# Two-layer encoder: query and key columns of the first four k tiles inside the first pieces, a first modulation unit on TensorE, copies of turned x on ScalarE

## The chip, the core and the metric

The kernel runs on one core of a Trainium2 chip. Its engines work from queues of their own, each in its written order: TensorE multiplies matrices into the accumulation memory (PSUM), VectorE and ScalarE do element-wise work, GpSimd a little, and SyncE (SP) issues nearly all transfers from the main memory. In the profile they are PE (and PEld for loading of weights into TensorE), DVE, ACT, POOL and SP. The metric is the device time of one execution in microseconds (us). Before the change the median of three executions was 2297.42 us (2294.97 to 2298.74).

## The reference

The program is an encoder trunk of two layers over 256 tokens of 2048 channels, all in float32. What matters here is the head of layer 0:

```python
mod = (c_act @ w_mod[l] + b_mod[l]).reshape(bn, 6, d)     # six vectors of 2048
h = layer_norm(x) * (1.0 + scale_m) + shift_m
proj = h @ w_in[l]                                        # 2048 x 4288
uv, q_c, kv_c, k_r, sb, sc, sh, ag = jnp.split(proj, IN_SPLITS, axis=-1)
y_a = gmlp_mixer(uv, ...)          # U and V, 512 columns each
y_b = mla_mixer(q_c, kv_c, k_r, ...)   # B: 704 columns, padded to 768
y_c = short_conv_mixer(sb, sc, sh, ...)  # E = sb (512), C = sc and sh (1024)
y_d = conformer_conv(ag, ...)      # D: 1024 columns
y = jnp.concatenate([y_a, y_b, y_c, y_d], axis=-1) @ w_out[l]
x = layer_norm(ALPHA * x + (1.0 + gate_m) * y, ...)
```

After that comes a gated feed-forward with a width-3 convolution (weights 2048 x 11264 and 5632 x 2048), and the same again for layer 1. Every weight is read once; the modulation alone reads 2048 x 12288 numbers a layer.

## The kernel before, in words

A **k tile** is 128 of the 2048 input channels; there are 16. The input projection multiplies each k tile of the weights with the same k tile of h, transposed (channels on the partitions, 256 tokens along the row; tiles hF), and sums over the 16.

**Modulation on VectorE.** The vectors mod are not made by TensorE. VectorE runs over w_mod, one k tile at a time: acc = w * c_act[k] + acc (mod_step, lines 246 and 248; tiles qacc, macc, sources wmod), and at the end TensorE sums acc over the partitions with products against a column of ones (mod_cols, result ps_mod), to which the bias bcol is added by a product with the identity matrix. ScalarE then copies the few columns out (line 205, and line 86 with +1 for scales).

**Layer 0 starts in five pieces** (PIECES: k tiles 0-1, 2-3, 4-7, 8-11, 12-15; function by_pieces). Shift and scale for a piece's channels are made first (mod_piece: units of 1 MB of w_mod), then h for that piece (line 1477 and line 86 in place on hF), then the piece's share of the products with the columns D, U, V and E, while VectorE makes the modulation of the next piece. The code of a piece has four steps; each does a quarter of D, and the first three one of U, V and E (function side), and between them calls some_mods, which issues the next piece's modulation units. D keeps its four accumulation banks (accD) through all pieces. U, V and E share the two banks that are left: at the end of a side, ScalarE copies both banks out (sums, line 1284; part, line 1289), and from the second piece on VectorE adds what was copied to the sum in SBUF (line 1290; in the last piece line 1286 directly).

**Plain and split products.** For k tiles 0 to 3 (PLAIN_KT = 4), and for U, V and E up to k tile 11, weights go straight from memory into TensorE as float32 (tiles wexact, loads on line 431); each such product shows as two TensorE records. Otherwise the weights (wraw, loads on line 439) and h are split in a high part (whi, hT: ScalarE, lines 453 and 473) and a low part (wlo: VectorE, lines 454 and 474), and three products are summed.

**After the pieces** group B runs over its 16 k tiles in 8 units of 2 (function group, all plain, tiles B_c), then C in the same manner; the attention of B is computed in between C's products. One unit is one call of stream, which issues the unit's loads, a number of w_mod steps for later use (RATES: 1.6 per unit for B; generator mods), and a number of VectorE jobs that wait in the list background (STEPS: 2 per unit for B; they are the 31 taps of D's convolution, line 903, with ScalarE's products of line 902).

**Buffers.** w_mod units, w_mod steps and wraw share four 1 MB tiles (rawp); wexact, whi and wlo share four and four half-MB tiles (splitp). SP issues loads in program order and waits at the first whose tile isn't free. The Tile framework orders each engine's instructions by its own estimate, so the order on an engine is not quite that of the code.

**The start.** x is loaded, normalised (ScalarE, line 86, tiles xn), turned by TensorE (line 1449, ps_xT), and copied into hF by ScalarE (line 1453) and VectorE (line 1455) in turns. At the same time VectorE runs the first piece's 16 modulation steps of 512 columns (four units of four k tiles).

Of the kernel before, what the change touches and what calls it, by code (L numbers as in the profile page):

```python
# [35 lines left out]
    dict(B=1.6, C=1.9, out=1.7, first=1.2, up=0.68, down=0.83),  # L36
# [4 lines left out]
    dict(B=2, C=2, up=2),  # L41
# [13 lines left out]
def encoder_kernel(ctx: ExitStack, tc: tile.TileContext, A: dict, consts: bass.AP, out: bass.AP):  # L55
# [195 lines left out]
    def mod_piece(l, ms, k0, nkt):  # L251
# [5 lines left out]
        units = []  # L257

        def unit(u):
# [9 lines left out]
            for k in range(nk):  # L269
                mod_step(acc, raw[:, k, :, :].rearrange("p m c -> p (m c)"), u * nk + k, u == 0 and k == 0)  # L270
# [4 lines left out]
        def sums():  # L275
            for i, m in enumerate(ms):
                mod_cols(l, m, k0, acc[:, i * width : (i + 1) * width])
# [198 lines left out]
    def group(w, c0, width, name, then, ntm=0, nk=2, hF=None, bg=0, spare=0):  # L476
# [48 lines left out]
        return KT // nk, load, products, end, bg  # L525

    def group2(w, c0, name, then, bg=0, spare=0):
# [23 lines left out]
        return KT // nk, load, products, lambda: then(box["c"]), bg  # L551

    def run(g):
        units, load, products, end, bg = g
        for u in range(units):
            stream(lambda: load(u), lambda item, u=u: products(item, u), bg)
        pending.append(end)
# [685 lines left out]
    def by_pieces(l, w_in, hF, between, mix_d, mix_u, mix_v, mix_b, mix_c, mix_e):  # L1243
# [4 lines left out]
        cols = {"U": C_UV, "V": C_UV + 512, "E": C_SB}  # L1248
# [22 lines left out]
        def side(g, parts, k0, nkt):  # L1271
            ps = [acc_tile(f"{g}{l}_{i}") for i in range(2)]
            for kt, part in parts:
                st, sp = kt == k0, kt == k0 + nkt - 1
                if g == "V":
                    ts = terms(kt, part)
                    for t in range(2):
                        for n, (w, x) in enumerate(ts):
                            mm(ps[t], x[:, t * P : (t + 1) * P], w, st and n == 0, sp and n == len(ts) - 1)
                else:  # L1280
                    chan_major(ps, kt, part, range(4), st, sp)
            for i in range(2):
                if k0 == 0:
                    act.copy(sums[g][i], ps[i])
                elif k0 + nkt == KT:
                    dve.tensor_tensor(out=sums[g][i], in0=ps[i], in1=sums[g][i], op=ALU.add)
                else:
                    part = tmp_tile("part")
                    act.copy(part, ps[i])
                    dve.tensor_tensor(out=sums[g][i], in0=part, in1=sums[g][i], op=ALU.add)  # L1290

        first = between(0)[1]
        first()
        for q, (k0, nkt) in enumerate(PIECES):
# [4 lines left out]
            def load(g, kt):  # L1299

                c0, width = (C_AG, 1024) if g == "D" else (cols[g], 512)
                nk = min(2048 // width, nkt)
# [17 lines left out]
            for s in range(4):  # L1320
# [114 lines left out]
    def normed_T(hF):  # L1435
# [3 lines left out]
        for t in range(2):  # L1439
# [4 lines left out]
            for q in range(4):  # L1444
# [7 lines left out]
                if q % 2 == 0:  # L1452
                    act.copy(dst, src)
                else:
                    dve.tensor_copy(dst, src)
# [151 lines left out]
```

## Time and profile before

| what | value |
|---|---|
| median of three executions | 2297.42 us (2294.97 to 2298.74) |
| the profiled execution, its own time | 2298.88 us |
| its span in the profile | 2297.1 us |
| TensorE, VectorE, ScalarE busy | 97%, 78%, 47% of the span |
| read from memory | 601 MB |

The profiled execution lies 1.5 us over the median, and its span 1.8 us under its own time; the 1.8 us are around the span and not in any view. Times in the views count from the start of the span. A row of grouped instructions gives the line, the engine, the operation, what is written and read with the shape, the count, the busy time, the mean of one, and the idle time of the engine just before them with what ended it. In a table of stretches, each engine has its busy us with the number of instructions that began there, and behind them stand the granted TensorE clock (1.00 is full), the busy share of the 16 transfer engines (transfers that overlap can take it over 1) and the rate in GB/s. TensorE's busy time is that of records that overlap in a pipeline, so the mean of one is longer than its share of a dense stretch: the busy time divided by the count is used here.

### The profile page before, as it was taken

How to read it: one execution, taken by the hardware profiler on the slowest of the kernel's cores; microseconds unless marked ns; L12 is line 12 of the kernel's file. 1: busy time of each engine (PE TensorE's matmuls, PEld its weight loads, DVE VectorE, ACT ScalarE, POOL GpSimd, SP SyncE). 2: the span in 40 equal slices, each digit the busy share in tenths (PEclk: the TensorE clock that was granted, in tenths of full speed). 3: DMA queues.
4: the chain of work that ended last, by engine and by line, in shares of the span. 5: the costliest groups of instructions: out<-in, count | busy, mean ns of one | idle time of the engine just before them, and what ended most of it. 6: DMA issues, size and time to landing. Idle time of an engine off the chain costs nothing.

```text
span 2297.1 us, 31478 instructions
## 1 busy us (share of the span) xinstructions
PE 2238.4 (97%) x12387; PEld 1934.1 (84%) x12387; DVE 1790.7 (78%) x2211; ACT 1071.6 (47%) x1597; POOL 34.4 (1%) x65
## 2 busy tenths in 40 slices
PE   6899999999999999999999999999999999999998
PEld 4688886798888888888789999889888888888886
DVE  6878987778888888998977899796676565565676
ACT  2235742335454544544455435545454454454553
POOL 2000000000000000000000000000000000000000
PEclk9899999999999999999999999999999999999999
DMA  9999788777889888898857677875665555555554
GB/s 344 362 340 343 271 321 333 263 278 279 317 303 335 292 326 318 303 354 307 311 186 260 202 238 252 291 260 185 249 243 202 193 178 197 192 193 185 188 195 147
DMA packets 228717, 605.21 MB, mean 263 GB/s; under 512 B 14660, under 2 KB 27188, under 8 KB 210900
## 3 DMA queue, kind: packets, MB, share of 16 engines
q1 hardware_dynamic: 227784, 602.30, 73.7%
q8 instruction: 97, 1.59, 0.3%
q0 software_dynamic: 784, 0.90, 0.1%
q14 instruction: 52, 0.43, 0.0%
HBM read 601.05 MB, written 2.10 MB: 263 GB/s over the span
## 4 chain that ended last, share of the span: by engine, by line
PE 89%; DVE 5%; DMA 3%; issue 1%; ACT 1%; SPq 0%; POOL 0%; DVEq 0%; POOLq 0%; ACTq 0%
PE g_c L83 21%; PE v_c L83 21%; PE d L83 20%; PE o L83 8%; PE D_c L83 4%; PE C_c L83 4%; PE B_c L83 3%; DMA wmod<-in_w_mod_dram 2%; PE U_c L83 1%; DVE wlo L454 1%; PE U L83 1%; PE E L83 1%; PE ps_mod L83 1%; PE E_c L83 1%; DVE qacc L248 1%
## 5 line engine op out<-in xcount | busy, mean ns | idle before, releaser
L453 ACT CAST whi<-wraw 128x1024 fp32r<-128x1024 f32 (+1 forms) x632 | 643.6, 1043 | 780.4 <-PE g_c L83 210.0
L454 DVE TENSOR_TENSOR wlo<-wraw,whi 128x1024 fp32r<-128x1024 f32 (+1 forms) x632 | 750.6, 1214 | 292.2 <-ACT whi L453 278.3
L83 PE MATMUL d<-whi,a 128*128 128x512 f32 x1344 | 390.6, 392 | 0.9 <-ACT whi L453 0.9
L248 DVE SCALAR_TENSOR_TENSOR macc<-wmod,cact,macc 128x2048 f32<-128x2048 f32 (+2 forms) x174 | 353.8, 2033 | 32.3 <-DMA wmod<-in_w_mod_dram 31.7
L83 PE MATMUL v_c<-hT,whi 128*128 128x512 f32 (+1 forms) x1456 | 343.1, 383 | 0.0
L83 PE MATMUL g_c<-hT,whi 128*128 128x512 f32 (+1 forms) x1344 | 313.3, 380 | 0.0
L83 PEld LDWEIGHTS v_c<-hT,whi 128*128 128x128 f32 x1456 | 264.6, 189 | 48.5
L83 PEld LDWEIGHTS d<-whi,a 128*128 128x128 f32 x1344 | 253.2, 189 | 54.6 <-ACT whi L453 2.2
L83 PEld LDWEIGHTS g_c<-hT,whi 128*128 128x128 f32 x1344 | 243.4, 189 | 43.2
L83 PE MATMUL d<-wlo,a 128*128 128x512 f32 x672 | 234.4, 392 | 1.6 <-DVE wlo L454 1.6
L83 PE MATMUL v_c<-hT,wlo 128*128 128x256 f32 x1400 | 190.7, 283 | 0.0
L83 PEld LDWEIGHTS v_c<-hT,wlo 128*128 128x128 f32 x1400 | 183.1, 191 | 6.6
L83 PE MATMUL g_c<-hT,wlo 128*128 128x256 f32 x1280 | 175.8, 283 | 0.0
L83 PEld LDWEIGHTS g_c<-hT,wlo 128*128 128x128 f32 x1280 | 168.2, 191 | 5.9
L83 PEld LDWEIGHTS d<-wlo,a 128*128 128x128 f32 x672 | 127.0, 189 | 30.3 <-DVE wlo L454 3.9
L473 ACT CAST a<-g 128x512 fp32r<-128x512 f32 x132 | 80.8, 619 | 91.0 <-PE d L83 89.3
L83 PE MATMUL o<-whi,a 128*128 128x512 f32 x384 | 112.4, 398 | 0.8 <-ACT whi L453 0.8
L474 DVE TENSOR_TENSOR a<-g,a 128x512 fp32r<-128x512 f32 x132 | 87.7, 685 | 9.5 <-ACT a L473 9.5
L83 PEld LDWEIGHTS o<-whi,a 128*128 128x128 f32 x384 | 73.1, 191 | 17.5 <-ACT whi L453 1.2
L83 PE MATMUL D_c<-hT,whi 128*128 128x256 f32 x432 | 82.0, 290 | 2.8 <-ACT hT L473 2.3
L248 DVE SCALAR_TENSOR_TENSOR qacc<-wmod,cact,qacc 128x1024 f32<-128x1024 f32 (+1 forms) x75 | 80.3, 1070 | 2.6 <-DMA wmod<-in_w_mod_dram 0.5
L1364 DVE SCALAR_TENSOR_TENSOR u<-g,pf,u 128x254 f32<-128x254 f32 (+1 forms) x176 | 73.5, 476 | 3.0 <-ACT u L86 3.0
(371 smaller groups left out, 2603.7 us busy)
## 6 DMA issues: line engine op xcount, KB each, us to landing
wraw<-in_ffn_w_up_dram SPq DMA_DIRECT2D x168, 1024.0 KB, 5.0
wmod<-in_w_mod_dram SPq DMA_DIRECT2D x134, 1024.0 KB, 6.2
wraw<-in_ffn_w_down_dram SPq DMA_DIRECT2D x88, 1024.0 KB, 5.2
wraw<-in_w_in_dram SPq DMA_DIRECT2D x33, 1024.0 KB, 6.9
wmod<-in_w_mod_dram SPq DMA_DIRECT2D x64, 512.0 KB, 9.2
wraw<-in_w_out_dram SPq DMA_DIRECT2D x26, 1024.0 KB, 6.7
wmod<-in_w_mod_dram SPq DMA_DIRECT2D x32, 768.0 KB, 6.6
wexact<-in_w_in_dram SPq DMA_DIRECT2D x46, 512.0 KB, 7.4
```

The lines of the kernel that those rows point to most:

```text
L83: pe.matmul(o, lhsT, rhs, start=start, stop=stop, skip_group_check=True)
L248: i = dve.scalar_tensor_tensor(out=acc, in0=w, scalar=col, in1=acc, op0=ALU.mult, op1=ALU.add)
L453: act.copy(hi[:, :m], r)
L454: i = dve.tensor_tensor(out=lo[:, :m], in0=r, in1=hi[:, :m].bitcast(F32), op=ALU.subtract)
L473: act.copy(hi, src)
L474: dve.tensor_tensor(out=lo, in0=src, in1=hi.bitcast(F32), op=ALU.subtract)
L1364: dve.scalar_tensor_tensor(out=u[:, sh:], in0=x[:, : S - sh], scalar=col(k, j), in1=u[:, sh:], op0=ALU.mult, op1=ALU.add)
```

## The change

Four things change, all before the end of group B of layer 0, with three numbers of the plan.

1. **Group B's first four k tiles join the first two pieces.** The step that did V does "VB" where the piece is plain: after V, B's 768 columns of the piece's two k tiles are loaded (two transfers of 384 KB a piece, line 440 in the new file, behind V's load and two of the next piece's modulation loads, ahead of E's) and multiplied (12 products a piece, three banks of four blocks, between V's and E's). Their sums stay in SBUF (sumB); group starts with unit 2 of 8 and copies them into its accumulation banks first.
2. **Sides start from their earlier sum.** side now takes its banks one after the other. From the second piece on, ScalarE copies the sum so far into the bank (act.copy(o, total)), TensorE accumulates on top, and ScalarE copies the bank back. VectorE's additions (lines 1286 and 1290, 24 of 128x512) are gone. U's last piece is not copied back: its GELU reads the banks (mix_u moves from behind the pieces into the last one).
3. **The first modulation unit goes to TensorE.** Of the first piece's four units, unit 0 (4 k tiles x 2 vectors x 2 column blocks) becomes 16 products of a 128x128 block of w_mod with a column of c_act, into a bank (modfirst), which then also takes the bias and the sums of VectorE's remaining 12 steps.
4. **All eight copies of turned x are ScalarE's** (line 1468 in the new file).

Of the plan: each of the first three steps of the last piece calls next(mods), which is one w_mod step (1 MB and one VectorE pass of 128x2048); B's rate becomes 1.634 (6 units, 9.8 steps, where 8 units gave 12.8); B's background jobs per unit become 3 (18 where there were 16).

How the order moves is shown at three places. **VectorE at the start** (qacc is the modulation sum, hF the turned x, ps_xT the transposes, bcol the bias); before:

```order
L248 SCALAR_TENSOR_TENSOR qacc<-wmod,cact,qacc 128x512 x4
L1455 COPY hF_116<-ps_xT 128x4x128
L248 SCALAR_TENSOR_TENSOR qacc<-wmod,cact,qacc 128x512
L1455 COPY hF_118<-ps_xT 128x4x128
L248 SCALAR_TENSOR_TENSOR qacc<-wmod,cact,qacc 128x512
L1455 COPY hF_116<-ps_xT 128x4x128
L248 SCALAR_TENSOR_TENSOR qacc<-wmod,cact,qacc 128x512 x2
L1455 COPY hF_118<-ps_xT 128x4x128
L248 SCALAR_TENSOR_TENSOR qacc<-wmod,cact,qacc 128x512
L142 COPY bcol_106<-ps_rows 128x96
L248 SCALAR_TENSOR_TENSOR qacc<-wmod,cact,qacc 128x512 x4
L1477 TENSOR_SCALAR hF_115<-hF_115,mod_1_0_276,mod_0_0_270 128x256
```

and now (rs is the factor of the normalisation, which xn waits for):

```order
L583 SCALAR_TENSOR_TENSOR rs_in_145<-mv_in_143,rs_in_145 128x1
L583 SCALAR_TENSOR_TENSOR rs_in_188<-mv_in_186,rs_in_188 128x1
L246 TENSOR_SCALAR qacc<-wmod,cact 128x512
L248 SCALAR_TENSOR_TENSOR qacc<-wmod,cact,qacc 128x512 x10
L142 COPY bcol_106<-ps_rows 128x96
L248 SCALAR_TENSOR_TENSOR qacc<-wmod,cact,qacc 128x512
L1490 TENSOR_SCALAR hF_115<-hF_115,mod_1_0_289,mod_0_0_284 128x256
```

The four copies have left, 12 modulation steps stand where 16 did, and rs stands ahead of all of them (before, three steps stood ahead of it).

**VectorE in the third piece** (k tiles 4-7; qacc here is the fourth piece's modulation, wlo the low part of D's weights); before:

```order
L246 TENSOR_SCALAR qacc<-wmod,cact 128x1024
L248 SCALAR_TENSOR_TENSOR qacc<-wmod,cact,qacc 128x1024 x7
L1290 TENSOR_TENSOR sumU<-part,sumU 128x512 x2
L248 SCALAR_TENSOR_TENSOR qacc<-wmod,cact,qacc 128x1024 x6
L454 TENSOR_TENSOR wlo<-wraw,whi 128x1024
L1290 TENSOR_TENSOR sumV<-part,sumV 128x512
L454 TENSOR_TENSOR wlo<-wraw,whi 128x1024
```

and now:

```order
L246 TENSOR_SCALAR qacc<-wmod,cact 128x1024
L248 SCALAR_TENSOR_TENSOR qacc<-wmod,cact,qacc 128x1024
L483 TENSOR_TENSOR hT<-hF_116,hT 128x2x256 x2
L248 SCALAR_TENSOR_TENSOR qacc<-wmod,cact,qacc 128x1024 x12
L463 TENSOR_TENSOR wlo<-wraw,whi 128x1024 x2
L248 SCALAR_TENSOR_TENSOR qacc<-wmod,cact,qacc 128x1024 x2
```

The additions that waited for U's and V's banks between the steps are gone; the same 14 steps still stand ahead of the first wlo.

**SP in the last piece** (k tiles 12-15; wraw of 2x1024 is D's weights, of 4x512 that of U, V and E); before:

```order
L439 DMA wraw<-in_w_in_dram 128x2x1024
L439 DMA wraw<-in_w_in_dram 128x4x512 x2
L439 DMA wraw<-in_w_in_dram 128x2x1024
L439 DMA wraw<-in_w_in_dram 128x4x512
```

and now:

```order
L448 DMA wraw<-in_w_in_dram 128x2x1024
L448 DMA wraw<-in_w_in_dram 128x4x512
L358 DMA wmod<-in_w_mod_dram 128x2048
L448 DMA wraw<-in_w_in_dram 128x4x512
L358 DMA wmod<-in_w_mod_dram 128x2048
L448 DMA wraw<-in_w_in_dram 128x2x1024
L448 DMA wraw<-in_w_in_dram 128x4x512
L358 DMA wmod<-in_w_mod_dram 128x2048
```

Two w_mod steps now stand ahead of D's second and E's weights, in the same four tiles.

Behind that, up to the end of layer 0's ffn_w_up, a few neighbouring instructions change places on the engines; from there on every engine's order is the old one. The diff, cut to its core:

```diff
-    dict(B=1.6, C=1.9, out=1.7, first=1.2, up=0.68, down=0.83),
+    dict(B=1.634, C=1.9, out=1.7, first=1.2, up=0.68, down=0.83),
-    dict(B=2, C=2, up=2),
+    dict(B=3, C=2, up=2),
...
-    def mod_cols(l, m, k0, acc):
+    def mod_cols(l, m, k0, acc, begun=None):
-        ps = ms_tile("ps_mod")
-        mm(ps[:, 0:n], ident, bcol[l][:, m * KT + k0 : m * KT + k0 + n], True, False)
+        ps = ms_tile("ps_mod") if begun is None else begun
+        mm(ps[:, 0:n], ident, bcol[l][:, m * KT + k0 : m * KT + k0 + n], begun is None, False)
...
+        begun = acc_tile("modfirst") if k0 == 0 else None
...
             for k in range(nk):
-                mod_step(acc, raw[:, k, :, :].rearrange("p m c -> p (m c)"), u * nk + k, u == 0 and k == 0)
+                kt = u * nk + k
+                if begun is None or u > 0:
+                    mod_step(acc, raw[:, k, :, :].rearrange("p m c -> p (m c)"), kt, kt == (0 if begun is None else nk))
+                    continue
+                for i in range(n):
+                    for j in range(nkt):
+                        o = begun[:, i * nkt + j : i * nkt + j + 1]
+                        mm(o, raw[:, k, i, j * P : (j + 1) * P], cact[:, kt : kt + 1], k + i + j == 0, False)
...
+        skip = 0 if begun is None else PLAIN_KT // nk
...
-            if u == 0:
+            if u == skip:
                 box["c"] = [acc_tile(f"{name}_c{i}") for i in range((ncm + 1) // 2)]
+                if begun is not None:
+                    for bank, part in zip(box["c"], begun):
+                        act.copy(bank, part)
...
         def side(g, parts, k0, nkt):
-            ps = [acc_tile(f"{g}{l}_{i}") for i in range(2)]
-            for kt, part in parts:
...
+            for i, total in enumerate(sums[g]):
+                o = acc_tile(f"{g}{l}_{i}")
+                if k0 > 0:
+                    act.copy(o, total)
+                for kt, part in parts:
...
+                if g == "U" and k0 + nkt == KT:
+                    u_banks.append(o)
                 else:
-                    part = tmp_tile("part")
-                    act.copy(part, ps[i])
-                    dve.tensor_tensor(out=sums[g][i], in0=part, in1=sums[g][i], op=ALU.add)
+                    act.copy(total, o)
+            if u_banks and g == "U":
+                mix_u(u_banks, None)
...
-                if s < 3:
-                    g = "UVE"[s]
+                for g in ("U", "VB", "E", "")[s] if exact else ("U", "V", "E", "")[s]:
                     load(g, k0)
-                    some_mods((0.5, 0.85, 1.0)[s])
+                    some_mods((0.5, 0.85, 1.0, 1.0)[s])
                     side(g, [(kt, loaded[(g, kt)]) for kt in range(k0, k0 + nkt)], k0, nkt)
+                if k0 + nkt == KT and s < 3:
+                    next(mods)
         mix_d(accD, None)
-        mix_u(sums["U"], None)
...
-        run(group(w_in, C_Q, 768, f"B{l}", mix_b, hF=hf, bg=STEPS[l]["B"]))
+        run(group(w_in, C_Q, 768, f"B{l}", mix_b, hF=hf, bg=STEPS[l]["B"], begun=sums["B"]))
...
-                if q % 2 == 0:
-                    act.copy(dst, src)
-                else:
-                    dve.tensor_copy(dst, src)
+                act.copy(dst, src)
```

More of the change, by code (lines that the diff above doesn't have):

```diff
@@ L523, in end @@
             then(box["c"], box["t"])
-        return KT // nk, load, products, end, bg
+        return range(skip, KT // nk), load, products, end, bg
     def group2(w, c0, name, then, bg=0, spare=0):
@@ L549, in load @@
             return weights(w, u * nk, nk, c0, 512, False, spare if u == 0 else 0)
-        return KT // nk, load, products, lambda: then(box["c"]), bg
+        return range(KT // nk), load, products, lambda: then(box["c"]), bg
     def run(g):
         units, load, products, end, bg = g
-        for u in range(units):
+        for u in units:
             stream(lambda: load(u), lambda item, u=u: products(item, u), bg)
```

32 lines of the change are left out of this document (15 added, 17 removed).

## The prediction

> **What bounds the kernel now.** I read the page first, then busy time by stage, then who waited for whom, then the stretches with a low clock.
>
> ```profile
> span 2297.1 us, 31478 instructions
> PE 2238.4 (97%) x12387; PEld 1934.1 (84%) x12387; DVE 1790.7 (78%) x2211; ACT 1071.6 (47%) x1597; POOL 34.4 (1%) x65
> ```
>
> TensorE is busy 97% of the span, so the kernel is a queue of TensorE work; a gain must come from the 59 us in which it is not busy (2297.1 - 2238.4), or from stretches at a low clock. By stage (start; first two pieces; third; fourth; last piece with the rest of D; group B; C):
>
> ```profile
> 0.00:32.50 32.50, 9.99 (x51) 7.96 (x51) 20.71 (x38) 12.10 (x19) 8.95 (x27) 0.93 0.98 327
> 32.50:53.00 20.50, 20.50 (x79) 16.22 (x80) 11.52 (x17) 3.94 (x9) 0.00 (x0) 0.87 1.06 378
> 53.00:85.00 32.00, 25.36 (x104) 18.66 (x102) 27.50 (x32) 7.69 (x15) 5.32 (x10) 0.89 0.98 350
> 85.00:122.50 37.50, 34.94 (x172) 28.80 (x173) 29.63 (x28) 7.93 (x12) 0.00 (x0) 0.91 1.01 370
> 122.50:160.00 37.50, 35.96 (x205) 29.74 (x205) 30.53 (x31) 10.48 (x18) 0.00 (x0) 1.00 0.97 354
> 160.00:190.70 30.70, 30.40 (x232) 29.24 (x231) 23.24 (x22) 11.62 (x14) 0.00 (x0) 1.00 0.79 280
> 190.70:235.20 44.50, 44.17 (x217) 38.86 (x215) 41.61 (x40) 30.07 (x71) 2.56 (x5) 1.00 1.01 369
> 235.20:310.00 74.80, 74.51 (x359) 62.81 (x359) 66.24 (x82) 43.86 (x106) 1.80 (x1) 1.00 0.77 279
> ```
>
> Length less TensorE's busy time: the start costs 22.5 us, the second piece (53 to 85) 6.6, the third and fourth 4.1 together; from 160 on TensorE is full. The transfers are the reverse: full (0.97 to 1.06) up to 160 and in group B, 0.79 in the last piece. So the pieces are bound by transfers with TensorE idle in places, group B by both, the last piece by TensorE alone. The waits inside the pieces, and the half clock that follows a gap:
>
> ```profile
> PE D_c L83 <- DVE wlo L454: 3.4, 2, 2.6
> PE V L83 <- DMA wexact<-in_w_in_dram: 2.7, 2, 2.4
> PE D_c L83 <- ACT hT L473: 2.0, 1, 2.0
> PE E L83 <- DMA wexact<-in_w_in_dram: 2.0, 1, 2.0
> 27.60:37.60 10.00, 7.92 (x24) 6.83 (x25) 7.42 (x12) 1.02 (x3) 0.00 (x0) 0.50 1.09 356
> 67.75:72.30 4.55, 4.55 (x7) 1.97 (x8) 4.44 (x4) 0.01 (x1) 0.00 (x0) 0.62 0.94 325
> 75.15:79.00 3.85, 3.85 (x10) 3.07 (x11) 3.84 (x5) 0.00 (x0) 0.00 (x0) 0.56 1.03 397
> 110.00:113.00 3.00, 3.00 (x14) 3.00 (x15) 3.00 (x4) 0.00 (x0) 0.00 (x0) 0.50 1.02 401
> ```
>
> In the second piece V waits 2.4 us and E 2.0 us for weights. The granted clock falls after the gaps: 4.55 us at 0.62 behind V's wait lose 1.7 us, 3.85 at 0.56 behind E's 1.7, 3.0 at 0.50 behind the wait for wlo 1.5.
>
> **The change part by part.** The sum is made against the profiled execution, 2298.88 us.
>
> *a) The start.* D's first product began at 32.49 us.
>
> ```profile
> 14.37 0.49 DVE L246 TENSOR_SCALAR qacc<-wmod,cact 128x512 f32<-128x512 f32 x1 [0.27 <-DMA wmod<-in_w_mod_dram]
> 16.34 0.22 DVE L569 SCALAR_TENSOR_TENSOR rs_in<-mv_in,rs_in 128x1 f32<-128x1 f32 x2
> 17.76 2.33 DVE L248 SCALAR_TENSOR_TENSOR qacc<-wmod,cact,qacc 128x512 f32<-128x512 f32 x3 [0.53 <-DMA wmod<-in_w_mod_dram]
> L248 DVE SCALAR_TENSOR_TENSOR qacc<-wmod,cact,qacc 128x512 f32<-128x512 f32 x14 | 10.5, 748 | 0.8 <-DMA wmod<-in_w_mod_dram 0.5
> L86 ACT ACTIVATE xn<-x,rs_in 128x512 f32<-128x512 f32 x8 | 6.1, 808 | 12.3 <-DVE rs_in L569 12.3
> L1455 DVE COPY hF<-ps_xT 128x512 f32<-128x512 f32 x4 | 2.8, 688 | 0.3 <-PE ps_xT L1449 0.3
> L1453 ACT COPY hF<-ps_xT 128x512 f32<-128x512 f32 x4 | 2.3, 576 | 0.1
> L83 PE MATMUL ps_mod<-onesR,qacc 128*128 128x1 f32 x48 | 5.5, 245 | 0.0
> 17.40 3.00 PE L1449 MATMUL ps_xT<-cst,xn 128*128 128x128 f32 x12 [12.79 <-ACT xn L86]
> 29.64 1.87 PE L83 MATMUL ps_mod<-onesR,qacc 128*128 128x1 f32 x8 [2.42 <-DVE qacc L248]
> 30.69 0.16 ACT L205 COPY mod<-ps_mod 128x2 f32<-128x2 f32 x1 [6.13 <-PE ps_mod L83]
> 32.49 6.36 PE L83 MATMUL D_c<-hF,wexact 128*128 128x256 f32 x16
> ```
>
> VectorE's 12 remaining steps can't start before unit 1 has landed (17.76); 12 x 0.75 = 9.0 us and the bias's turn bring it to about 27 instead of 29.6 us, the four copies (2.8 us) no longer between. The 16 products on TensorE are 32 records of one column like the sums': 32 x 5.5 / 48 = 3.7 us from 14.37, done at 18.0, hidden as TensorE waits for x until 17.4, so the first transpose is late by 0.6. ScalarE then has 8 copies x 0.58 and about 6 of the 8 normalisations x 0.76 ahead of it from about 18.6: 9.2 us, to 27.8. It is now the later one. From the first modulation copy (30.69) to D was 1.8 us, so D starts at about 29.7: **-2.8 us**. Bounds: -3.5 (rs comes earlier, its row now ahead of three steps), -1 (ScalarE's queue longer by its four copies' waits).
>
> *b) First and second piece.* B's row prices the moved products:
>
> ```profile
> L83 PE MATMUL B_c<-hF,wexact 128*128 128x256 f32 x192 | 41.9, 379 | 0.0
> DVE hF L1477 <- ACT mod L86: 9.8, 3, 8.4
> ```
>
> 24 of 96 products are 48 records x 0.218 = 10.5 us, 5.2 in each piece. The first piece was full, so its 5.2 stand on the path. In the second they stand between V and E, where E's wait (2.0) and its low clock (1.7) go. V's wait stays: its load is queued on SP behind modulation units whose tiles VectorE must free, and VectorE stood 8.4 us at line 1477 for the first piece's end, which moves by a) and the 5.2 us with TensorE. So the third piece's modulation comes by 10.5 - 3.7 = 6.8 us later, less a): +4.0. The transfers give the same: 1.57 MB (four of 393 KB) at 378 GB/s are 4.2 us in stretches that were full. **+6.8 us**; bounds: +2.7 (V's wait and low clock go as well), +10.5 (no wait goes).
>
> *c) Third and fourth piece.* The additions leave VectorE:
>
> ```profile
> DVE sumU L1290 <- ACT part L1289: 7.5, 5, 3.2
> L1290 DVE TENSOR_TENSOR sumU<-part,sumU 128x512 f32<-128x512 f32 x6 | 4.1, 691 | 7.5 <-ACT part L1289 7.5
> L1289 ACT COPY part<-E 128x512 f32<-128x512 f32 x6 | 3.5, 587 | 9.6 <-PE E L83 9.6
> ```
>
> Six additions a group, and 7.5 us in which VectorE, in order, stood at U's and could not run the steps behind it. The wlo that TensorE waited for (3.4 us, with 1.5 of low clock) stood behind those steps. What is late next is D's second weights themselves, as the transfers are 4 us later by b). I take half, **-2.5 us**; bounds 0 and -4.9. The new copies into the banks (0.59 each) lie beside the other bank's products (8 records x 0.218 = 1.7 us in the second piece, 16 or 3.5 us after); without that cover they would cost some 1.3 us a bank, with the copy out.
>
> *d) The last piece.* Three w_mod steps go where transfers are at 0.79 and VectorE at 23.2 of 30.7 us: hidden, 0; bounds 0 and the slower rival. U's additions and copies gone change nothing on TensorE, which is full.
>
> *e) Group B* loses the 10.5 us from a stretch in which TensorE was busy 44.17 of 44.5: **-10.5 us**. The three copies into its banks lie beside D's last products. Transfers lose 1.57 MB and three steps there, so they stay no bound.
>
> *f) Behind B.*
>
> ```profile
> L903 DVE TENSOR_TENSOR convD<-convD,prodD 128x1020 f32<-128x1020 f32 (+12 forms) x13 | 15.5, 1189 | 0.8 <-ACT prodD L902 0.5
> PE ps_mod L83 <- DVE macc L248: 1.8, 1, 1.8
> ```
>
> In the new order 10 taps, not 15, stand ahead of the first use of B's sums on VectorE, so five more stand between the attention's VectorE steps in C: 5 x 1.19 = 5.9 us of VectorE, mostly beside C's products (TensorE had 74.5 of 74.8). And an earlier TensorE meets the modulation of the output projection, where it waited 1.8 us already, earlier. I take **+2.5 us** for both; bounds 0 and +7.7.
>
> Sum: -2.8 + 6.8 - 2.5 + 0 - 10.5 + 2.5 = **-6.5 us**, 2292.4 for the profiled execution. That execution lies 1.5 us over the median of the three, so against 2297.42 it is **2291**.
>
> **The rivals.** *No gain (25%).* The pieces absorb little: the transfers are late by b) through both later pieces, c) gives 0 to 3 us and E's wait returns in another place, b) at its upper bound: -2.8 + 10.5 - 1.5 - 10.5 + 2.5 = -1.8, so about 2296. For it speaks the transfer share of 1.0 in every piece, against it that 4.2 us of transfers can't cost 10.5.
>
> *More gain by the clock (17%).* D's first products ran at 0.50 from 32.49 to 37.6, behind a TensorE that had been idle 2.42 us before the sums and little used before. With products from 14.4 on and transposes until about 28, the idle stretch shrinks to a microsecond or two, and D could start at full clock: 5.1 us x 0.5 = -2.6 us, and with c) at its full 4.9, -11.5 in all, 2286. [...]
>
> *Slower (13%).* The last piece. SP is in order and the four 1 MB tiles are shared; before, all five weight loads were issued by 158.1:
>
> ```profile
> 144.17 13.95 SPq L439 DMA_DIRECT2D wraw<-in_w_in_dram x5
> 170.95 1.05 ACT L453 CAST whi<-wraw 128x1024 fp32r<-128x1024 f32 x1 [1.83 <-PE U L83]
> ```
>
> Now D's second weights wait for a tile that U's splits free, E's for a tile that a w_mod step on VectorE frees. If they land later than about 172 (splitting came at 170.95), TensorE waits: 3 MB at 370 GB/s are 8.5 us, and a half clock behind it 1.7: -6.5 + 10.2 = +3.7, about 2301. Against it: the stage's transfers are at 0.79, and 12.8 us lie between the last of those issues and that split.
>
> **How the numbers follow.** Forecast 45% (own range 2288 to 2294), no gain 25%, more gain 17%, slower 13%. A measurement can tell 0.2%, 4.6 us, from no change: faster is below 2292.8. That takes five sixths of the forecast (38), all but a little of more gain (16) and a little of no gain (3): 0.57. Slower than 2302 by more than 0.2%: most of the slower rival: 0.12. Same: 0.31. The range 2285 to 2299 leaves out 6% below and 12% above.
>
> **What would show it.** a) D's first product at 29.7, ScalarE's last copy of x the last releaser. b) The third piece's modulation sums, which stood right behind E's products, at about 84, V still waiting, E not. c) No wait for wlo over 1 us near 110. d) No wait for whi or wlo from 160 to 190. e) B's products at 144 records, their last at about 226 to 229. f) C without gaps over 1 us. I am wrong if B ends later than 232, or if the lead there is lost before 450.

## The result and the profile after

The changed kernel takes 2291.20 us (median of 8 runs, 2286.72 to 2292.99), the kernel before, run beside it, 2298.08 (8 runs, 2294.97 to 2300.34). The ratio is 0.9971, with a 95% interval of 0.9961 to 0.9981: 0.29% or 6.7 us faster. The profiled execution took 2292.73 us, its span is 2290.9 us, 6.2 less than before.

So the time came out as forecast (2291). The way there did not: the start lost where it was to gain, and the pieces gained what it lost. The head of the changed kernel's page:

```profile
span 2290.9 us, 31562 instructions
...
PE 2244.5 (98%) x12419; PEld 1939.4 (85%) x12419; DVE 1769.2 (77%) x2179; ACT 1097.5 (48%) x1642; POOL 33.5 (1%) x65
```

Its busy time by stage (length, then for PE, PEld, DVE, ACT and POOL busy us and instructions, then granted clock, transfer share, GB/s):

```profile
53.00:85.00 32.00, 31.28 (x142) 25.00 (x141) 20.20 (x20) 13.22 (x25) 5.08 (x10) 1.00 0.91 329
85.00:122.50 37.50, 33.93 (x175) 27.32 (x174) 26.33 (x24) 13.90 (x24) 0.00 (x0) 0.95 1.05 390
122.50:160.00 37.50, 37.03 (x210) 30.76 (x208) 27.98 (x26) 14.91 (x25) 0.00 (x0) 1.00 1.04 390
160.00:190.70 30.70, 30.70 (x233) 29.48 (x234) 20.18 (x17) 19.01 (x29) 0.00 (x0) 1.00 0.85 284
190.70:228.00 37.30, 37.30 (x195) 33.45 (x194) 35.24 (x36) 26.02 (x58) 2.84 (x5) 1.00 0.98 365
228.00:300.00 72.00, 68.58 (x320) 56.81 (x320) 68.35 (x85) 47.13 (x117) 1.02 (x1) 0.98 0.78 289
```

From 53 to 85 us TensorE is now busy 31.28 of 32.00 (25.36 before) at full clock (0.89 before). Of its waits from 53 to 160 us, those for E's weights (2.0 before) are gone, those for wlo (3.4 before) nearly so, and V's longest is 0.7 (2.4 before):

```profile
PE D_c L83 <- ACT hT L482: 1.6, 1, 1.6
PE V L83 <- DMA wexact<-in_w_in_dram: 1.4, 2, 0.7
PE D_c L83 <- DVE wlo L463: 0.3, 2, 0.2
```

In C it is the other way round: 68.58 of 72.00. The same window of the kernel before:

```profile
228.00:300.00 72.00, 71.71 (x348) 60.87 (x346) 67.56 (x83) 46.19 (x117) 1.80 (x1) 1.00 0.78 281
```

How far ahead the changed kernel is, read from the first record at seven places of TensorE's timeline:

| place on TensorE | before | after | difference |
|---|---|---|---|
| D's first product | 32.49 | 35.62 | +3.1 |
| modulation sums for the third piece | 80.36 | 85.80 | +5.4 |
| for the fourth | 120.80 | 123.99 | +3.2 |
| for the last | 157.50 | 159.48 | +2.0 |
| end of group B (sums ps_ss) | 235.00 | 225.84 | -9.2 |
| first product of the output projection | 326.68 | 321.95 | -4.7 |
| layer 1, first product of U | 1209.7 | 1203.4 | -6.3 |

**The start.** Rows of the changed kernel's timeline on TensorE (start, busy us, operation, count, idle time before and what ended it):

```profile
12.82 0.98 PE L83 MATMUL modfirst<-cact,wmod 128*128 128x1 f32 x4 [8.21 <-DMA wmod<-in_w_mod_dram]
14.37 6.13 PE L83 MATMUL modfirst<-cact,wmod 128*128 128x1 f32 x28 [0.57 <-DMA wmod<-in_w_mod_dram]
20.36 1.95 PE L1465 MATMUL ps_xT<-cst,xn 128*128 128x128 f32 x8
...
33.20 0.58 PE L83 MATMUL modfirst<-bcol,cst 128*128 128x2 f32 x2 [0.25 <-ACT mod L205]
33.65 0.99 PE L83 MATMUL modfirst<-onesR,qacc 128*128 128x1 f32 x4
35.62 5.36 PE L83 MATMUL D_c<-hF,wexact 128*128 128x256 f32 x16 [0.98 <-ACT hF L86]
```

The first and the last of the eight copies on ScalarE's:

```profile
21.49 0.59 ACT L1468 COPY hF<-ps_xT 128x512 f32<-128x512 f32 x1 [5.84 <-PE ps_xT L1465]
...
30.19 0.59 ACT L1468 COPY hF<-ps_xT 128x512 f32<-128x512 f32 x1 [0.60 <-PE ps_xT L1465]
```

The unit's records take 6.13 / 28 = 0.22 us each, not 0.115, so the transposes begin at 20.36, three us later than before. Behind them ScalarE needs 9.3 us for its copies (21.49 to 30.78). The bias and the sums follow in turn, and once more late: scale's bias lies in the same bank as shift's sums, so TensorE waits at 33.20 for the copy out.

**C.** What TensorE waited for between 220 and 345 us in the changed kernel (total, times, longest):

```profile
PE ps_rkv L83 <- DVE dgB L1083: 2.4, 1, 2.4
PE ps_ss L83 <- ACT sqB L1054: 1.0, 1, 1.0
```

VectorE's timeline there (kvr and dgB are steps of the attention on B's sums, convD is a tap of D's convolution):

```profile
230.59 0.48 DVE L1061 TENSOR_SCALAR kvr<-B_c,pm 128x256 f32<-128x256 f32 x1
230.98 1.17 DVE L917 TENSOR_TENSOR convD<-convD,prodD 128x980 f32<-128x980 f32 x1
232.07 0.48 DVE L1061 TENSOR_SCALAR kvr<-B_c,pm 128x256 f32<-128x256 f32 x1
232.46 1.17 DVE L917 TENSOR_TENSOR convD<-convD,prodD 128x976 f32<-128x976 f32 x1
...
238.20 0.48 DVE L1083 TENSOR_SCALAR dgB<-cst,rr 128x128 f32<-128x128 f32 x2
```

B's products end at 225.84, and dgB, which TensorE needs for ps_rkv, is ready at 238.68: 12.8 us. Before, it was 235.00 to 242.67, 7.7 us:

```profile
242.19 0.48 DVE L1069 TENSOR_SCALAR dgB<-cst,rr 128x128 f32<-128x128 f32 x2
```

From the end of B to the output projection it now takes 96.1 us instead of 91.7.

### The profile page after: what moved, and what is told of

The parts are those of the page before. It is cut to its first block, busy times and chain, and to the rows that moved or that the text cites. A ratio compares the mean times of both kernels' runs of the same rounds, so it can differ in the third digit from the quotient of the medians.

```text
span 2290.9 us, 31562 instructions
## 1 busy us (share of the span) xinstructions
PE 2244.5 (98%) x12419; PEld 1939.4 (85%) x12419; DVE 1769.2 (77%) x2179; ACT 1097.5 (48%) x1642; POOL 33.5 (1%) x65
## 4 chain that ended last, share of the span: by engine, by line
PE 86%; DVE 6%; DMA 4%; ACT 2%; issue 2%; POOL 0%; SPq 0%; DVEq 0%; ACTq 0%; POOLq 0%
PE g_c L83 21%; PE v_c L83 21%; PE d L83 20%; PE o L83 5%; PE C_c L83 4%; PE D_c L83 3%; DMA wmod<-in_w_mod_dram 2%; PE B_c L83 2%; DVE wlo L463 1%; PE U_c L83 1%; PE E L83 1%; PE E_c L83 1%; DMA wraw<-in_w_in_dram 1%; PE ps_mod L83 1%; DVE qacc L248 1%
## 5 line engine op out<-in xcount | busy, mean ns | idle before, releaser
L248 DVE SCALAR_TENSOR_TENSOR qacc<-wmod,cact,qacc 128x1024 f32<-128x1024 f32 (+1 forms) x71 | 77.3, 1089 | 10.7 <-DMA wmod<-in_w_mod_dram 8.6
```

The source lines that it names most:

```text
L248: i = dve.scalar_tensor_tensor(out=acc, in0=w, scalar=col, in1=acc, op0=ALU.mult, op1=ALU.add)
```

## The experiments

All are kernels of their own, with the kernel before run beside them; the ratios are to that. Places and waits are each read from one profiled execution. An interval is 95%. "After" in a diff is the changed kernel.

### The start: which of its two edits costs

The changed kernel with the copies divided between ScalarE and VectorE again:

```diff
-                act.copy(dst, src)
+                if q % 2 == 0:
+                    act.copy(dst, src)
+                else:
+                    dve.tensor_copy(dst, src)
```

> The changed kernel with VectorE again making every second copy of turned x (part 4 undone). Theory 1 (TensorE at half clock): the 32 records of the first modulation unit take 7 us as in the changed kernel and transposes begin at 20.4; from there ScalarE has 4 copies less, 2.3 us; D's first product at 33 to 34 instead of 35.6. Theory 2 (ScalarE's eight copies alone make the start late): D at 32.5 or earlier, as before the change. For the end: if a later D is carried to the end, 2 us less than the changed kernel (2289); if the pieces absorb it (V waits again for its weights), no difference beyond 1 us.

The changed kernel with the first unit on VectorE again:

```diff
-        begun = acc_tile("modfirst") if k0 == 0 else None
+        begun = None
```

> The changed kernel with the first modulation unit back on VectorE (part 3 undone), ScalarE still making all copies. Theory 1: transposes begin at 17.4 again, 3 us earlier, and D's first product at 32 to 33. Theory 2: ScalarE's queue is what counts, D stays at 35 or later. The clock will tell as well: with less TensorE work before D, D should start at half clock. End by carrying: 2288 to 2289; absorbed: 2291.

And with both undone:

> The changed kernel with parts 3 and 4 undone: the start as before the change (D at 32.5), the rest as changed. If the 3 us by which the changed kernel starts later are carried to the end: 2288. If they are absorbed because V and E in the second piece then wait longer for weights: 2291, with V's wait back at about 2 us.

| kernel | D's first product | end of B | ratio | median, us |
|---|---|---|---|---|
| after | 35.62 | 225.84 | 0.9971 (0.9961 to 0.9981) | 2291.20 |
| copies divided again | 36.95 | 226.68 | 0.9987 (0.9976 to 0.9997) | 2291.83 |
| unit on VectorE again | 30.65 | 220.62 | 0.9949 (0.9934 to 0.9964) | 2285.99 |
| both undone | 32.87 | 221.94 | 0.9963 (0.9948 to 0.9977) | 2288.27 |

TensorE's timeline in the kernel with the unit on VectorE again:

```profile
17.22 5.05 PE L1465 MATMUL ps_xT<-cst,xn 128*128 128x128 f32 x20 [12.61 <-ACT xn L86]
...
27.82 1.84 PE L83 MATMUL ps_mod<-onesR,qacc 128*128 128x1 f32 x8
...
30.65 6.08 PE L83 MATMUL D_c<-hF,wexact 128*128 128x256 f32 x16
```

The transposes start at 17.22 again, and D at 30.65, earlier than the 32 to 33 expected. With the copies divided it came at 36.95, later than either theory had it. The unit on TensorE costs D 4.1 us (36.95 against 32.87) or 5.0 (35.62 against 30.65); the copies on ScalarE gain 1.3 or 2.2. What D starts late by is carried along: over the four kernels D's start spreads by 6.3 us and the end of B by 6.1. The ratios go the same way, 0.22 and 0.24 percentage points for the unit, though the intervals within each pair overlap. The copies on ScalarE, the second theory's limit, are the part of the start that gains; without the unit ahead of the transposes they end at 26.89 (30.78).

### Why the unit takes 7 us

Idle products of ones by ones on TensorE ahead of the start, into a bank of their own, change nothing but its activity. First 28, ahead of the turning of c:

```diff
+    wps = ms_tile("warm")
+    for i in range(28):
+        mm(wps[:, 0:128], ones, ones, True, True)
```

> The changed kernel with 28 products of a matrix of ones with itself on TensorE from 2.7 us, whose result nobody reads. Theory 1: they end at 10 to 12 us, bring TensorE to full clock, the first modulation unit's 32 records take about 3.7 us instead of 7, transposes begin at about 18, D at about 33, and D's own first products run at 0.22 instead of 0.43 us a record, 1.7 us more. Theory 2: the records of one column cost 0.22 us each at any clock, D stays at 35.6. End by carrying: 2287; absorbed: 2290 to 2291.

The time did not move: 2290.64 us, ratio 0.9977 (0.9966 to 0.9989), D at 35.51. But the busy time by stretches of this kernel says why:

```profile
12.00:14.00 2.00, 0.67 (x4) 0.61 (x4) 1.97 (x4) 0.00 (x0) 0.77 (x2) 0.78 1.08 355
14.00:16.00 2.00, 1.75 (x9) 1.75 (x9) 0.42 (x4) 1.52 (x2) 0.56 (x1) 0.50 1.10 341
16.00:18.00 2.00, 2.00 (x11) 2.00 (x11) 0.31 (x1) 0.00 (x0) 0.00 (x0) 0.50 1.10 343
```

The first four records took 0.67 us (0.98 without the idle products); then the granted clock fell to 0.50, and the other 28 took 6.13 us, to the digit what they took in the changed kernel. There the clock column says 1.00 for the same stretch, but the first change of the clock in that trace is recorded at 39.0 us, and the records take 0.22 us each, as here at 0.50: that 1.00 is not a measurement. So I filled the gap, with 16 more idle products right behind the turning of c:

```diff
+    for i in range(16):
+        mm(wps[:, 128:256], ones, ones, True, True)
```

> The changed kernel with 28 idle products ahead of the turning of c (as before) and 16 more right behind it, so that TensorE has no gap before the first modulation products. Theory 1 (those products are slow because TensorE is at half clock): the 28 records that took 6.13 us take 28 x 0.119 = 3.3 us at a granted clock of 1.00, the first transpose starts near 17.7 rather than 20.36; ScalarE's eight copies then need 9.3 us to about 28, and D starts at about 33 (35.62 in the changed kernel): 2.5 us less, near 2288.7. Theory 2 (their cost is not the clock): still 0.22 us a record at a granted 1.00, D at 35.5, near 2291. If the clock falls again in spite of the products, 0.50 stands in the rows and nothing is decided.

Its timeline on TensorE:

```profile
11.44 3.84 PE L83 MATMUL warm<-onesR 128*128 128x128 f32 x32
15.12 4.71 PE L83 MATMUL modfirst<-cact,wmod 128*128 128x1 f32 x32
19.69 1.95 PE L1471 MATMUL ps_xT<-cst,xn 128*128 128x128 f32 x8
```

And its busy time by stretches:

```profile
14.20:16.00 1.80, 1.80 (x19) 1.80 (x17) 0.16 (x1) 1.43 (x2) 0.43 (x1) 1.00 1.08 331
16.00:18.00 2.00, 2.00 (x18) 2.00 (x17) 0.60 (x2) 0.00 (x0) 0.00 (x0) 0.86 1.11 347
18.00:20.40 2.40, 2.40 (x13) 2.40 (x14) 2.14 (x3) 0.00 (x0) 0.00 (x0) 0.50 1.09 351
```

Up to 17.4 us the starts of the unit's records lie 0.11 us apart; behind that, at the granted 0.50, they lie 0.21 apart, as they do all through the unit in the changed kernel. (The count in a stretch is of all records that overlap it, not only of those that began there, so the spacing is taken from the records' starts.) So the half clock is what made the unit slow, as the first theory had it. The second half of that theory failed: the idle products held the unit's first record until 15.12, 0.7 us behind the landing of most of its weights, the clock fell again within the unit, the transposes came 0.7 us earlier and D 0.7 (34.96), and the time stayed (2289.04 us, 0.9971, 0.9960 to 0.9982). The 44 idle products at the front alone did not keep the clock up (0.50 from 17.4 us).

A third kernel took the unit off TensorE, and put idle products ahead of the turning of c, behind it, and behind each four transposes:

```diff
+    wps = acc_tile("warm")
+    for i in range(28):
+        mm(wps[:, 0:128], ones, ones, True, True)
...
+    for i in range(28):
+        mm(wps[:, 128:256], ones, ones, True, True)
...
-        begun = acc_tile("modfirst") if k0 == 0 else None
+        begun = None
...
+                for i in range(2):
+                    mm(wps[:, 256:384], ones, ones, True, True)
```

> The changed kernel with its first modulation unit on VectorE again, and idle products on TensorE: 28 ahead of the turning of c, 28 behind it, and two with each group of four transposes, 16 in all. Theory 1 (the head is lost to the half clock too): D's 16 records take 3.6 us rather than 6.1, the 8 sums ahead of them 0.95 rather than 1.84, U starts near 33.3 (36.57 without the idle products) and 3.3 us are carried to the end: near 2282.7. Rival (the transfers of the first two pieces bound them): U starts earlier, but the weights of V and E don't, the third piece's sums stay at 80.9, and the time at 2286.

Its timeline on TensorE:

```profile
27.92 0.58 PE L83 MATMUL ps_mod<-bcol,cst 128*128 128x2 f32 x4 [1.72 <-DVE bcol L148]
28.49 1.05 PE L83 MATMUL ps_mod<-onesR,qacc 128*128 128x1 f32 x8
...
30.53 5.37 PE L83 MATMUL D_c<-hF,wexact 128*128 128x256 f32 x16 [0.25 <-ACT hF L86]
```

And the stretch in which D began:

```profile
31.00:34.00 3.00, 3.00 (x8) 2.35 (x8) 2.55 (x4) 0.00 (x0) 0.00 (x0) 0.52 1.07 356
```

The clock held (the sums took 1.05 us, not 1.84), but VectorE's steps were then the last to come, with a wait of 1.72, and behind it the clock fell for D after all. U started 0.8 us earlier, not 3.3, and the time, 2286.37 us, ratio 0.9953 (0.9937 to 0.9968), is that without the idle products. It is also the rival's time, but that confirms neither theory: the head start was never there to be carried.

### What the pieces and group B pay

The changed kernel without B in the pieces, with as many modulation steps:

```diff
-    dict(B=1.634, C=1.9, out=1.7, first=1.2, up=0.68, down=0.83),
+    dict(B=1.225, C=1.9, out=1.7, first=1.2, up=0.68, down=0.83),
...
-    dict(B=3, C=2, up=2),
+    dict(B=2, C=2, up=2),
...
-                for g in ("U", "VB", "E", "")[s] if exact else ("U", "V", "E", "")[s]:
+                for g in ("U", "V", "E", "")[s] if exact else ("U", "V", "E", "")[s]:
...
-        run(group(w_in, C_Q, 768, f"B{l}", mix_b, hF=hf, bg=STEPS[l]["B"], begun=sums["B"]))
+        run(group(w_in, C_Q, 768, f"B{l}", mix_b, hF=hf, bg=STEPS[l]["B"]))
```

> The changed kernel without B in the pieces: B has its 8 units again (2 jobs and 1.225 modulation steps each, so that the steps in the last piece stay). Theory (the pieces take B in cheaply): B's move is worth +2.3 in the first two pieces and -11.1 in group B, of which C gives some 4 back, so without it the kernel is 5 to 9 us slower than the changed one, 2296 to 2300, with the third piece's modulation sums near 83 (85.80) and the end of B near 235 (225.84). Rival (the transfers make the pieces pay for all of it): the third and fourth pieces come earlier by what B took, some 7 us, and the time stays within 2 us of 2291.

Neither 5 to 9 us slower nor any faster: 2291.46 us, 0.9977 (0.9966 to 0.9989). The last piece's sums come 6.5 us earlier than with B (153.03), the end of B 3.9 later (229.75), and the output projection starts at the same time (321.58, against 321.95). Its stretch of C has no gap:

```profile
228.00:300.00 72.00, 71.98 (x341) 60.72 (x340) 64.84 (x82) 44.40 (x108) 1.02 (x1) 0.98 0.72 264
```

So B's products cost the pieces 6 of the 10.4 us that group B saves, and C gave back the other 4: in this change B's move was worth nothing that the runs can tell.

The other way, the sides' sums added by VectorE again:

```diff
-                if k0 > 0:
-                    act.copy(o, total)
...
-                if g == "U" and k0 + nkt == KT:
-                    u_banks.append(o)
-                else:
-                    act.copy(total, o)
+                if k0 == 0:
+                    act.copy(total, o)
+                elif k0 + nkt == KT:
+                    dve.tensor_tensor(out=total, in0=o, in1=total, op=ALU.add)
+                else:
+                    part = tmp_tile("part")
+                    act.copy(part, o)
+                    dve.tensor_tensor(out=total, in0=part, in1=total, op=ALU.add)
...
```

> The changed kernel with the sides' sums added by VectorE again (a bank is copied out by ScalarE and added by VectorE from the second piece on, in the last piece added directly), all else as changed. Theory (VectorE's additions held the steps behind them, and so the low parts of D's weights): the fourth and last pieces' sums, at 123.99 and 159.48, come 2 to 4 us later, the wait for wlo near 110 is back, and the time is 2293.5 to 2295. Rival (VectorE has room, and the gain of these pieces came from the order of loads): within 1 us of 2291.

It takes 2302.24 us, ratio 1.0020 (1.0006 to 1.0034): slower than the kernel before, and 11 us slower than the changed one, three times the most that was expected. (It isn't quite the old order: a side's banks are still taken one after the other, and B's products stand ahead; U's GELU is behind the pieces again.) What TensorE waited for from 53 to 160 us:

```profile
PE D_c L83 <- DVE wlo L463: 5.3, 2, 3.1
PE D_c L83 <- ACT hT L482: 2.4, 1, 2.4
PE ps_mod L83 <- DVE qacc L248: 1.5, 1, 1.5
```

And its third and fourth piece by busy time:

```profile
85.00:122.50 37.50, 30.34 (x148) 24.67 (x147) 32.76 (x34) 9.14 (x15) 0.00 (x0) 0.85 1.00 361
122.50:160.00 37.50, 34.52 (x183) 28.29 (x183) 27.11 (x28) 9.86 (x16) 0.00 (x0) 0.96 0.95 330
```

The waits for wlo are back, the clock is at 0.85, and TensorE is busy 30.34 of 37.50. The sums for the third, fourth and last piece come 2.0, 7.0 and 10.7 us later than in the changed kernel.

Last, the kernel before with the sides' change alone (as in the diff of the change, with the start, group B and its plan as before):

> The kernel before with the change to the sides alone (banks taken one after the other, begun with a copy of the earlier sum by ScalarE, U's last banks read directly): B has all its units, no modulation step in the last piece, the start as before. Theory (the sides carry the whole gain, B's move costs the pieces what it saves in group B and the rest is lost in C): the same time as with the sides and B's move together and the old start (2288.27), within 2 us; the last modulation sums near 150 (157.50 before), the end of B near 225 to 227, out_proj near 317. Rival (both are needed: the sides' gain shows in the third piece only with B's products ahead of it): 2293 or more.

2288.31 us, ratio 0.9961 (0.9949 to 0.9974). That is what the sides and B's move give together with the old start (0.9963), and no less than the whole change. The theory holds: **the sides carry the gain.** No run takes the sides' change apart in the old order (banks one after the other, no additions, U's GELU earlier); with B in the pieces, the run before shows it for the additions, with the GELU's place. Its second and third piece:

```profile
53.00:85.00 32.00, 24.58 (x108) 18.91 (x107) 25.71 (x28) 11.98 (x22) 5.61 (x10) 0.94 0.99 361
85.00:122.50 37.50, 37.20 (x207) 31.50 (x208) 28.77 (x27) 13.23 (x22) 0.00 (x0) 0.96 1.04 389
```

Its last piece's sums come at 150.98, 6.5 us earlier than before, from a D that began 0.9 later: 7.4 us. About half of that are waits: V, E, hT and wlo together cost 10.1 us from 53 to 160 before, and V, E and hT 6.7 here:

```profile
PE E L83 <- DMA wexact<-in_w_in_dram: 3.1, 1, 3.1
PE D_c L83 <- ACT hT L482: 2.0, 1, 2.0
PE V L83 <- DMA wexact<-in_w_in_dram: 1.6, 1, 1.6
```

The rest is the clock: 0.89 and 0.91 of these two stages are 0.11 x 32 + 0.09 x 37.5 = 6.9 us of lost clock, 0.94 and 0.96 are 3.4.

### What C gives back

Two jobs a unit in group B instead of three, on the kernel with the unit on VectorE:

```diff
-    dict(B=3, C=2, up=2),
+    dict(B=2, C=2, up=2),
```

> The changed kernel with its first modulation unit on VectorE, as one run before it (2285.99), and in group B two background jobs a unit again instead of three; nothing else. Theory 1 (taps of D's convolution, 1.17 us each, stand between the attention's steps on VectorE and hold TensorE in C): two taps instead of six stand between B's first step on VectorE (kvr) and dgB, so dgB is ready some 4 us earlier, and from the end of B's products to the first product of the output projection it takes 92 us instead of 94.9 (91.8 where B isn't moved): near 2283. Theory 2 (the time between is set by something else that an earlier B meets, VectorE's modulation steps or the transfers): the 94.9 stay, 2286.

The first part came as expected: TensorE no longer waits for dgB. The rest did not: the time is 2290.69 us, 0.9967 (0.9954 to 0.9979), no better than with three jobs, and from the end of B to the output projection it takes 96.7 us, not 92 (94.9 with three jobs). Among TensorE's waits there a new one stands first, for one of the attention's next steps:

```profile
PE ps_qr L83 <- DVE qc L1114: 2.3, 1, 2.3
```

So the taps alone are not it; VectorE is still busy 37.02 of 37.30 us in group B. Two modulation steps fewer in group B, on top of that:

```diff
-    dict(B=1.634, C=1.9, out=1.7, first=1.2, up=0.68, down=0.83),
+    dict(B=1.3, C=1.9, out=1.7, first=1.2, up=0.68, down=0.83),
```

> The run with two background jobs a unit and the modulation unit on VectorE, with group B's modulation steps at 1.3 a unit instead of 1.634, so that two steps of 2.35 us go from B to behind it. Theory 1 (VectorE, busy 36.5 of 37.3 us in group B, hands its backlog to C): no tap stands between rr and dgB, C takes about 91.5 us, 1 to 2 us less than with 1.634, near 2282. Theory 2 (C's VectorE is as full, 67 of 72 us, so what is moved there is waited for there or in the output projection): no gain or a loss, 2283 to 2287, with a longer stretch from C's end to the next norm.

This kernel has the lowest median: 2283.17 us (5 runs, 2282.21 to 2284.18), ratio 0.9938 (0.9926 to 0.9951), 8 us under the changed kernel and clear of it; the interval overlaps that of the kernel with the unit on VectorE (0.9934 to 0.9964). Group B and C in it:

```profile
190.70:228.00 37.30, 37.30 (x190) 32.60 (x188) 33.85 (x44) 25.39 (x64) 3.27 (x5) 1.00 1.03 394
228.00:300.00 72.00, 72.00 (x341) 61.43 (x342) 68.84 (x75) 45.51 (x106) 0.00 (x0) 1.00 0.79 278
```

VectorE is busy 33.85 us in group B (36.50 with the unit on VectorE and 1.634 steps), and TensorE has 72.00 of 72.00 in C. The output projection begins at 309.42, 90.2 us behind the first of B's ps_ss sums (96.7 with the old number of steps). Part of it is lost later: the first norm behind the output projection makes TensorE wait 3.3 us (0.8 at a time before), and of 6.1 us at the start of that projection (309.42 against 315.51 with 1.634 and three jobs) 2.4 are left at the end of the two profiled executions (spans of 2282.0 and 2284.4). A part of the lead is the start, too: D began at 28.91 here, in the same order of instructions, with eight sums that took 1.05 us and began at 26.87 (1.84 us and 27.82 in the kernel with the unit on VectorE and three jobs).

The last run takes B's move out of this kernel (eight units, 0.975 steps each):

> The fastest run so far (2283.17: the changed kernel with its modulation unit on VectorE, two jobs a unit and 1.3 modulation steps a unit in group B) without B in the pieces: B has 8 units, with 0.975 steps each, so that group B holds the same 7.8 steps. Theory 1 (B's move is worth some 4 us once VectorE's backlog no longer takes them in C): the end of B comes 3 to 4 us later, near 224 to 225 (221), the output projection begins near 313 to 315 (309.42), and the time is 2286 to 2288. Theory 2 (the gain was the lower rate's alone, and B's move is worth nothing in itself): 2283 again, the output projection near 310.

2289.29 us, 0.9968 (0.9956 to 0.9980), with the end of B at 226.61 and the output projection at 318.13. So the lower rate alone is not what was gained; B's move is worth 0.3%, 6 to 7 us, as soon as VectorE has room for what follows it. That is more than I expected; up to 1.9 us of it are D's start (30.77 against 28.91).

## Why the prediction was right, and where it was not

The time was right: 2291 forecast and measured. The terms were not all right, and that their misses offset each other so closely is luck. The start (5.9 us) and C (1.9) came out worse than forecast, the pieces (b 4.5, c 1.0), group B (0.6) and what lies behind the output projection (1.6) better.

- **a) The start, -2.8 forecast, +3.1 measured.** The failed step is "32 records x 5.5 / 48 = 3.7 us ... hidden". It took the mean of 48 records, 0.115 us, that all ran at a granted 1.00, the sums of the last three pieces (from 80 to 159 us). The row that fitted stood in the same fence: eight sums at the start in 1.87 us, 0.234 each, at half clock (0.50 from 27.60 to 37.60 us). With it the unit takes 7.5 us, and the transposes are late by three. The second step, ScalarE's 9.2 us behind them, measured 9.3. The third, 1.8 us from the first modulation copy to D, became 2.6, since the two sums now share a bank; with the unit on VectorE, and no shared bank, it is 1.8 again. The bounds (-3.5 to -1) did not hold it: they knew nothing of a half clock.
- **b) First and second piece, +6.8 forecast, +2.3 measured** from D's first product to the third piece's sums (47.87 us before, 50.18 after). E's wait and low clock went, as forecast; V's wait, forecast to stay, fell from 2.43 to 0.69 without a low clock behind it. B's products cover both waits: in the kernel without them in the pieces V waits 2.1 us and E 3.1. B alone costs +4.3 there, and the sides, which had no term there in the forecast, give back 2. The 4.3 is near the 4.2 that the forecast had from the transfers, and not the 6.8 that it took.
- **c) Third and fourth piece, -2.5 forecast, -3.5 measured,** and no wait for wlo over 1 us: right. But the sides are worth more in all than the bound of -4.9, which was the wait for wlo with its low clock: alone they give 7.4 us up to the last piece's sums, 2.2 of them in the first two pieces and 5.3 in the third and fourth, and 10.7 where B's products stand ahead of them.
- **d) The last piece, 0:** right, TensorE is busy 30.70 of 30.70; the slower rival did not come.
- **e) Group B, -10.5 forecast, -11.1 measured,** its end at 225.84 (226 to 229 forecast).
- **f) Behind B, +2.5 forecast, +4.4 measured,** within the bounds. The gap was to be under 1 us and is 2.4. Taps between the attention's steps, the first half of this term, do stand there, but with fewer of them the wait only moved. What shortened the stretch was two modulation steps fewer on top of that (96.7 to 90.2 us): VectorE's backlog sets it. Whether the steps alone would do, with three jobs, no run tells. The other half of the term was misread: TensorE's 1.8 us for macc stood at 496 us, behind the output projection, and it is 1.1 now.
- The lead of 4.7 us at the output projection became 6.3 in layer 1. I forecast nothing there. It was 5.0 within the output projection, 5.9 at the modulation sum for which TensorE had waited 1.8 us, and 6.3 right behind it. Why VectorE was nearer to ready with that sum no run tells.

Of the rivals, no gain was true of the change's main part: B's move paid nothing that the runs can tell, though for C's sake and not by a price in the pieces at its upper bound. More gain by the clock failed at its premise: earlier products on TensorE did not let D start at full clock (16 records in 5.36 us; 0.218 each would be 3.5), though TensorE had no gap of over 1 us from 14.37 us on. That a shorter idle stretch ahead of D would be enough was my estimate, and no run shows it.

What stays open: why the clock falls in one execution of a start and not in another with the same order, and how much of the best kernel's gain is that.

## What to carry to other kernels

Price a moved instruction from a row of the stage that it moves to, at that stage's clock, and not from a mean of other stages (here 0.22 us a record at 0.50, where the mean was 0.115). A step that is off the critical engine's path, such as an addition on an in-order VectorE, is worth what stands behind it (2302.24 us with the additions back, 2291.20 without), and in the kernel before TensorE's waits of 2.0 us and more were paid twice, once as a gap and once as half clock about its end. (The four of 2.0 to 2.6 us between 53 and 160 us end at 67.75, 75.15, 84.99 and 109.96, and the clock stands at 0.50 from 68.6 to 72.0, 75.4 to 78.8, 85.7 to 89.1 and 109.6 to 113.0; those under 1 us have none.) When products are moved ahead, ask who must be ready at their new end: here the saving was there, and VectorE's backlog ate it until its steps were moved too.

## What the runs showed of the hardware that I had not expected

TensorE's granted clock fell to 0.50 with no idle time ahead of it. With 44 idle products TensorE was busy without a gap from 2.70 to 21.6 us; the clock stood at 1.00 until 17.4, 2.3 us into products of a single column, and 0.50 from there through the transposes. With idle products of 128 columns between the transposes it read 1.00 up to 28 us and 0.92 from 28 to 31, and the eight sums took 1.05 us. So 2.3 us of one-column products without a gap did not keep it there, and elsewhere a fall came with a gap of 2 us (V's wait of 2.43 us before, 0.62 from 67.75 to 72.30). What the clock goes by no run tells.

In the changed kernel the clock column reads 1.00 ahead of the first recorded change (39.0 us), while the unit's 28 records take 6.13 us there, as they do with 28 idle products ahead at a recorded 0.50. Where it matters, the spacing of known records tells: with 44 idle products the one-column records start 0.21 us apart at a granted 0.50 and 0.11 at 1.00.
